# A hybrid decoder block on one core: rotary in place, another order of the second block's projections, and four smaller moves

## The chip, the cores and the metric

The kernel runs on one core of one Trainium2 chip. The metric is the device time of one execution in microseconds (us). The kernel before takes 2722.19 us, the median of three runs (2721.7 to 2723.53).

## The reference

The reference is one decoder layer for 2048 tokens of width 1024, in float32. What is touched here is the first projection and what hangs on it:

```python
h = modulate(rms_norm(x, g_pre_mix), shift_m, scale_m)
proj = h @ w_in
q_a, k_a, v_a, q_m, k_m, v_m, o_m, i_m, f_m, g_a, g_m = split(proj)
q_a, k_a = rope(q_a), rope(k_a)              # rotary on queries and keys
y_a = sliding_window_attention(q_a, k_a, v_a, sinks)   # 128-token window, softmax with a sink
qk_m = silu(causal_conv4([q_m, k_m]))
h_m = mlstm_chunkwise(q_m, k_m, v_m, i_m + b_i, f_m + b_f)
y_m = sigmoid(o_m) * head_layer_norm(h_m)
merged = sigmoid(g_a) * (y_a @ w_branch_attn) + sigmoid(g_m) * (y_m @ w_branch_mlstm)
x = x + gate_m * rms_norm(merged @ w_out)    # then the SwiGLU half, untouched here
```

`mod = c @ w_ada + b_ada` gives shifts, scales and gates. Rotary turns pairs of head columns: `[t1*cos - t2*sin, t2*cos + t1*sin]`. The mLSTM weights are `exp(d - m)` under a causal mask.

## The kernel before

The 2048 tokens are taken as two superblocks of 1024 (sb 0 and 1), each of two blocks of 512 tokens (b0 and b1; over the kernel they are blocks 0 to 3), each block of four token tiles of 128. Every float32 product is made of three fp32r matmuls: weights and activations are split into a high part (`whi`, `hl`) and a rest (`wlo`), by a copy on ScalarE (L259, L1353) and a subtraction on VectorE (L260, L1354).

A superblock's main list is written out in `superblock`: for b0 queries (C_Q, 512 columns), then keys, values and gate inputs together (264 columns), then the mLSTM values (`vm`, 512 columns); for b1 `vm` first, then queries, then keys/values. After it come the "pairs" (mLSTM q/k, output gate `om`, branch gates `ga` and `gm`), which take feature tiles of both blocks, then the outputs. `token_group` runs one such projection: four PSUM tiles `acc` (the pool has four), one per token tile, and an evacuation per tile (`evac_q` L781, `evac_kv` L805, `vm` L827: a ScalarE copy into an SBUF tile `tx`).

Beside the main list run streams: generators that were given a delay by `spawn` and are moved on by `tick` when a modelled clock has reached their time. They are the rotary tails `q_stream` and `k_stream`, the attention of a token tile (two streams, odd and even tiles), the gates' scans, the sums for the next activations, the modulation product `ada_stream`, and the mLSTM. The streams use four PSUM tiles `mix`. This fixes the order of each engine's instructions when the program is built; on the chip every engine works through its list in order and waits at semaphores.

The rotary path of a token tile: ScalarE copies the projection from `acc` to `raw` (`tx`). `rope` (L745 to L763) writes `raw*cos` to `y`, the swapped halves times sin to `z`, and adds `z` into `y`, five VectorE instructions. `q_stream` then has TensorE transpose `y` to a `mix` tile, and writes a high part (ScalarE, L771) and a rest (VectorE, L772) to `hi` and `lo`, which go to DRAM (`at_d`) by DMA; `k_stream` does the same for the keys (L796) into one tile `kk`. So a query tile takes five `tx` buffers (raw, y, z, hi, lo) and a key/value tile four. The pool has nine, given out in turn: the next tile waits for the release of the one whose buffer it gets. The attention of a token tile loads `at` from `at_d` (L908, two buffers), makes 24 score matmuls into four `mix` tiles, copies (L931), maxima, eight exponentials (L946), a reciprocal (L949), a scaling on GpSimd (L950), transposes, copies (L959), and the products with the values (PV), whose result ScalarE evacuates (L972).

In the mLSTM, `chunk_state` makes `wd` for a chunk by four VectorE instructions (add a per-row column, minimum with the mask `cneg`; L1022) and one exponential of 512 columns (L1023).

Of the kernel before, what the change touches and what calls it, by code (L numbers as in the profile page):

```python
# [71 lines left out]
def decoder_block(ctx: ExitStack, tc: tile.TileContext, a: dict, out: bass.AP, dbg=None):  # L72
# [27 lines left out]
    def mix_tile():  # L100
        return ps_mix.tile([P, 512], F32, tag="mix", name=nm("mix"))

    def tx(shape, dtype=F32):
        return tpool.tile(shape, dtype, tag="tx", name=nm("tx"), bufs=9)

    def tm(shape, dtype=F32):
        return mpool.tile(shape, dtype, tag="tm", name=nm("tm"), bufs=9)
# [202 lines left out]
    def token_group(srcs, nk, n, lhs, evac, pair_heads=False, stagger=1):  # L310

        acc = []
        srcs = list(srcs)
        held = []

        def make(si, k0, kc):
            def mms(wt):
                if not acc:
                    acc.extend(acc_tile() for _ in range(NT))
                held.append((wt, k0, kc))  # L320
                if len(srcs) - stagger <= si < len(srcs) - 1:
                    return
                for t in range(NT):
                    for w_, k0_, kc_ in held:
                        for j in range(kc_):
                            kk = k0_ + j
                            mm3(acc[t][:, :n], lhs(kk, t), (w_[0][:, j, :], w_[1][:, j, :]), kk == 0, kk == nk - 1)
                            yield
                    if si == len(srcs) - 1:
                        evac(t, acc[t])  # L330
                held.clear()
            return mms

        for si, (raw, view, k0, kc) in enumerate(srcs):
            yield piece(raw, view, [kc, n], make(si, k0, kc), pair_heads)
# [400 lines left out]
    def superblock(sb):  # L736
# [9 lines left out]
        def rope(raw, heads, b, t):  # L746
            sin, cos = tables[sb]
            t += (b % 2) * NT
            W = heads * HD
            raw = raw[:, :W]  # L750
            src = raw.rearrange("p (h u f) -> p h u f", u=2, f=32)
            cb = cos[:, t, :].unsqueeze(1).to_broadcast([P, heads * 2, 32])
            sb_ = sin[:, t, :].unsqueeze(1).to_broadcast([P, heads, 32])
            y = tx([P, W])
            z = tx([P, W])
            zz = z.rearrange("p (h u f) -> p h u f", u=2, f=32)
            yy = y.rearrange("p (h u f) -> p h u f", u=2, f=32)
            V.tensor_tensor(y.rearrange("p (h f) -> p h f", f=32), raw.rearrange("p (h f) -> p h f", f=32), cb, op=ALU.mult)
            V.tensor_tensor(zz[:, :, 0, :], src[:, :, 1, :], sb_, op=ALU.mult)
            V.tensor_tensor(zz[:, :, 1, :], src[:, :, 0, :], sb_, op=ALU.mult)  # L760
            V.tensor_tensor(yy[:, :, 0, :], yy[:, :, 0, :], zz[:, :, 0, :], op=ALU.subtract)
            V.tensor_tensor(yy[:, :, 1, :], yy[:, :, 1, :], zz[:, :, 1, :], op=ALU.add)
            return y  # L763

        def q_stream(b, t, y):
            yield L_ROPE
            pt = mix_tile()
            for j in range(GQ):
                transpose(pt[:, j * P:(j + 1) * P], y[:, j * P:(j + 1) * P])
            hi, lo = tx([P, 512], F32R), tx([P, 512], F32R)  # L770
            A.activation(hi, pt, AF.Copy, scale=HD ** -0.5)  # L771
            V.scalar_tensor_tensor(lo, pt, HD ** -0.5, hi.bitcast(F32), op0=ALU.mult, op1=ALU.subtract)  # L772
            for i, q in enumerate((hi, lo)):
                nc.sync.dma_start(at_d[b * NT + t][:, i * 512:(i + 1) * 512], q.bitcast(F32))
# [13 lines left out]
            nc.sync.dma_start(raw[:, :, 256:], w_in[:, C_IF:C_IF + 8].rearrange("(k p) c -> p k c", p=P))  # L788
            return raw

        def k_stream(n, y):
            yield L_ROPEK
            pt = mix_tile()
            transpose(pt[:, :P], y)
            kk = tx([P, 2, P], F32R)
            A.copy(kk[:, 0, :], pt[:, :P])  # L796
            V.tensor_tensor(kk[:, 1, :], pt[:, :P], kk[:, 0, :].bitcast(F32), op=ALU.subtract)
            for n_, u in ((n, 1), (n + 1, 0)):
                if n_ < S // P:
                    nc.sync.dma_start(at_d[n_][:, AT_K:AT_V].rearrange("p (i u k) -> p i u k", i=2, u=2)[:, :, u, :], kk.bitcast(F32))  # L800
# [16 lines left out]
            return evac  # L817

        def q_kv(b):
            yield from token_group(srcs_rows(w_in, KD, C_Q), KD, 512, lhs_h(b), evac_q(b), pair_heads=True)  # L820
            raw_kv = Raw(load_kv)
            yield from token_group([(raw_kv, (lambda r, j=j: r[:, j:j + 2, :]), j, 2) for j in range(0, KD, 2)], KD, 264, lhs_h(b), evac_kv(b))

        def vm(b):
            def evac(t, ps):
# [175 lines left out]
        def chunk_state(c):  # L1001
            b, t = b0 + c // NT, c % NT
            negm_d, mp, cl, ex = R["gates", b]
            cs = slice(t * P, (t + 1) * P)
            n_ = b * NT + t
            Cnew = c_tile(n_ + 1)
            km, qm = ld([MH, P]), ld([MH, P])
            nc.sync.dma_start(km, qk_d[b][:, 1, :, cs])
            nb = tm([P, MH, P])
            nc.sync.dma_start(nb, negm_d[:, cs].unsqueeze(0).to_broadcast([P, MH, P]))  # L1010
            nc.sync.dma_start(qm, qk_d[b][:, 0, :, cs])
            vc = vmt[n_ % 2]
            nc.sync.dma_start(vc[:, :, :MD], vm_d[b][:, t, :].rearrange("p (h d) -> p h d", h=MH))
            yield L_LOAD
            pk = mix_tile()
            for hh in range(MH):
                transpose(pk[:, hh * P:(hh + 1) * P], km[:, hh, :])
            kw = tm([P, MH, P])
            V.tensor_tensor(kw, pk.rearrange("p (h d) -> p h d", h=MH), ex[:, 0, t, :].unsqueeze(2).to_broadcast([P, MH, P]), op=ALU.mult)
            wd = tm([P, MH, P])  # L1020
            for hh in range(MH):
                V.scalar_tensor_tensor(wd[:, hh, :], nb[:, hh, :], cl[:, t, 0, hh:hh + 1], cneg, op0=ALU.add, op1=ALU.min)  # L1022
            A.activation(wd, wd, AF.Exp)  # L1023
            qs_ = None
            if n_ > 0:
                qs_ = tm([P, MH, P])
                G.tensor_tensor(qs_, nb, mp[:, :, t].unsqueeze(2).to_broadcast([P, MH, P]), op=ALU.add)
                A.activation(qs_, qs_, AF.Exp)
                G.tensor_tensor(qs_, qs_, qm, op=ALU.mult)
            R["w", c] = wd, qs_, km, qm, vc  # L1030
            yield L_KW
            pcn = [mix_tile() for _ in range(2)]
            for hh in range(MH):
                mm(pcn[hh // 2][:, (hh % 2) * 129:(hh % 2) * 129 + 129], kw[:, hh, :], vc[:, hh, :], True, True)
            for hh in range(MH):
                o = pcn[hh // 2][:, (hh % 2) * 129:(hh % 2) * 129 + 129]
                if n_ == 0:
                    V.tensor_copy(Cnew[:, hh, :], o)
                else:
                    V.scalar_tensor_tensor(Cnew[:, hh, :], C[n_][:, hh, :], ex[:, 2, t, hh:hh + 1], o, op0=ALU.mult, op1=ALU.add)  # L1040
# [238 lines left out]
            hps[b1] = spawn(hprep(b1), L_HP2)  # L1279

        yield start
        yield from q_kv(b0)
        yield lambda: attend(b0)
        if sb == 0:
            yield lambda: R.update(ada_m=[spawn(ada_stream([(2, "gate")], 5000.0))])
        yield from vm(b0)
        yield lambda: finish([hps[b1]])
        yield lambda: hps.update(t=spawn(hsums(("T2", "T4"))))
        yield from vm(b1)
        yield from q_kv(b1)  # L1290

        def start_f():
            finish([hps["t"]])
# [2 lines left out]
            attend(b1)  # L1296

        yield start_f
        pairs = [("qk", 0), ("om", 0), ("qk", 1), ("om", 1), ("qk", 2), ("ga", 0), ("qk", 3), ("ga", 1),
                 ("ga", 2), ("ga", 3), ("gm", 0), ("gm", 1), ("gm", 2), ("gm", 3)]  # L1300
        for i, (kind, p) in enumerate(pairs):
            parts = list(in_pair(kind, p))
            if i == 0:
                yield from parts[:3]
                yield lambda: finish([hps["t"]])
                parts = parts[3:]
            if i + 1 == len(pairs):
                yield from parts[:2]
                yield lambda: end_attention(NT)
                yield lambda: (load_y(b0, 0), load_g(b0, 0))  # L1310
                parts = parts[2:]
            yield from parts
            if (kind, p) == ("ga", 1):
                yield lambda: finish(convs + R["gs", b0] + R["gs", b1])
                yield lambda: spawn(mlstm(), L_ML)
        yield from outputs(b0)
# [550 lines left out]
```

## Time and profile before

| | before |
|---|---|
| median of three runs | 2722.19 us |
| the profiled execution | 2727.14 us |
| its span | 2725.4 us |
| TensorE (PE) busy | 2644.5 us, 97% |
| VectorE / ScalarE / GpSimd busy | 73% / 47% / 6% |
| DMA moved | 511.89 MB, mean 188 GB/s |

The profiled execution lies 4.95 us above the median of the runs, and its span 1.74 us below its own time. PE is busy for 97% of the span, so what can change the time is PE's work, its clock, and the 81 us in which it stands idle. About 33 us of these lie in the first 66 us (24.4) and the last 35 us (9.0) of the span.

### The profile page before, as it was taken

To read this page: it belongs to the slowest core of one execution; us is meant where nothing else is said; L and a number is where in the kernel's file an instruction comes from. 1 tells how busy PE (TensorE), PEld (TensorE's weight loads), DVE (VectorE), ACT (ScalarE), POOL (GpSimd) and SP (SyncE) were. 2 spreads that over 40 slices of the span, in tenths; PEclk is the share of its full clock that TensorE was granted. 3 is DMA by queue.
4 is the path that set the end of the run, shared out by engine and by line. 5 is a ranking of instruction groups with operands and counts; after the bars stand their busy time and mean duration, and the time that the engine had idled before them with its cause. 6 is when DMAs were issued, how large, how long until landed. Compare 5 with 4: busy or idle time off the path is not lost.

```text
span 2725.4 us, 35775 instructions
## 1 busy us (share of the span) xinstructions
PE 2644.5 (97%) x12310; PEld 2136.0 (78%) x12310; DVE 1999.1 (73%) x3954; ACT 1287.0 (47%) x2510; POOL 152.6 (6%) x189
## 2 busy tenths in 40 slices
PE   6999999999989899999999999999999999999998
PEld 4767778888877677888887888888877888888886
DVE  7959877866786988876587777776677676766456
ACT  5555743444755564334563443335554333333444
POOL 2010101100101010110000000000000000000000
PEclk8999999999999999999999999999999999999999
DMA  7755445697675554568765664436675332324566
GB/s 248 234 154 179 147 136 168 206 333 255 219 231 187 177 160 153 180 218 315 255 198 199 198 192 155 147 121 213 204 272 194 102 115 86 112 93 147 185 210 216
DMA packets 353639, 511.89 MB, mean 188 GB/s; under 512 B 25121, under 2 KB 213661, under 8 KB 348209
## 3 DMA queue, kind: packets, MB, share of 16 engines
q1 hardware_dynamic: 353456, 509.61, 56.6%
q8 instruction: 97, 1.59, 0.2%
q14 instruction: 86, 0.70, 0.1%
HBM read 357.12 MB, written 144.02 MB: 184 GB/s over the span
## 4 chain that ended last, share of the span: by engine, by line
PE 77%; DVE 7%; issue 4%; DMA 2%; ACT 2%; POOL 0%; SPq 0%; DVEq 0%; POOLq 0%; ACTq 0%
PE acc L204 54%; PE mix L204 22%; DVE hl L1354 1%; PE mix L209 1%; ACT hl L1353 1%; DMA at_d<-tx 1%; DMA raw<-as_d 1%; DVE tx L1132 1%; DMA raw<-in_w_ffn_down_dram 1%; DMA raw<-ws_d 0%; DVE w L1664 0%; DVE big L1354 0%; DVE big L552 0%; POOL rs L475 0%; DMA x1n<-tm 0%
## 5 line engine op out<-in xcount | busy, mean ns | idle before, releaser
L204 PE MATMUL acc<-big,hl 128*128 128x512 f32 x3936 | 947.7, 394 | 13.7 <-ACT tx L805 5.9
L204 PEld LDWEIGHTS acc<-big,hl 128*128 128x128 f32 x3936 | 732.8, 189 | 183.3 <-issue 10.2
L1353 ACT CAST hl<-raw 128x512 fp32r<-128x512 f32 x732 | 439.4, 621 | 500.5 <-PE acc L204 233.0
L1354 DVE TENSOR_TENSOR hl<-raw,hl 128x512 fp32r<-128x512 f32 x732 | 495.8, 694 | 193.6 <-ACT hl L1353 192.6
L204 PE MATMUL acc<-whi,big 128*128 128x512 f32 (+1 forms) x1280 | 380.8, 378 | 19.0 <-ACT big L518 8.4
L204 PEld LDWEIGHTS acc<-whi,big 128*128 128x128 f32 x1280 | 236.4, 192 | 65.9 <-ACT big L518 8.5
L204 PE MATMUL mix<-big,hl 128*128 128x512 f32 x1056 | 263.9, 390 | 1.6 <-ACT hl L1353 1.0
L204 PE MATMUL acc<-wlo,big 128*128 128x512 f32 (+1 forms) x640 | 241.8, 380 | 3.4 <-DVE wlo L260 3.4
L204 PE MATMUL acc<-hl,hl 128*128 128x512 f32 x1008 | 237.0, 393 | 4.7 <-DVE hl L1354 2.9
L204 PEld LDWEIGHTS mix<-big,hl 128*128 128x128 f32 x1056 | 197.7, 188 | 46.0 <-DVE hl L1354 1.8
L204 PEld LDWEIGHTS acc<-hl,hl 128*128 128x128 f32 x1008 | 187.1, 188 | 49.8 <-DVE hl L1354 8.4
L204 PE MATMUL mix<-hl,hl 128*128 128x512 f32 x792 | 183.2, 391 | 2.3 <-ACT hl L1353 1.4
L204 PEld LDWEIGHTS mix<-hl,hl 128*128 128x128 f32 x792 | 147.7, 188 | 37.0 <-DVE hl L1354 3.3
L260 DVE TENSOR_TENSOR wlo<-raw,whi 128x1024 fp32r<-128x1024 f32 (+1 forms) x96 | 108.8, 1133 | 71.8 <-ACT whi L259 65.1
L259 ACT CAST whi<-raw 128x1024 fp32r<-128x1024 f32 (+1 forms) x96 | 94.5, 985 | 128.6 <-PE acc L204 123.2
L204 PE MATMUL acc<-big,whi 128*128 128x512 f32 x512 | 154.9, 391 | 0.0
L204 PEld LDWEIGHTS acc<-wlo,big 128*128 128x128 f32 x640 | 123.1, 192 | 29.6 <-DVE wlo L260 5.1
L475 POOL TENSOR_TENSOR rs<-ms,nhalf 128x1 f32<-128x1 f32 (+1 forms) x56 | 42.7, 774 | 1642.4 <-DVE ms L473 1639.7
L204 PE MATMUL mix<-hcT4h,hl 128*128 128x512 f32 x352 | 117.6, 394 | 0.7 <-ACT hl L1353 0.7
L204 PE MATMUL acc<-hcT2h,hl 128*128 128x512 f32 x352 | 117.5, 394 | 0.0
L204 PEld LDWEIGHTS acc<-big,whi 128*128 128x128 f32 x512 | 95.7, 188 | 19.6
L204 PE MATMUL acc<-big,wlo 128*128 128x512 f32 x256 | 96.3, 392 | 0.0
(331 smaller groups left out, 3482.3 us busy)
## 6 DMA issues: line engine op xcount, KB each, us to landing
raw<-in_w_in_dram SPq DMA_DIRECT2D x48, 1024.0 KB
as_d<-w SPq DMA_DIRECT2D x154, 256.0 KB
raw<-as_d SPq DMA_DIRECT2D x70, 512.0 KB
raw<-in_w_ffn_gate_dram SPq DMA_DIRECT2D x22, 1024.0 KB
raw<-in_w_ffn_up_dram SPq DMA_DIRECT2D x22, 1024.0 KB
raw<-ws_d SPq DMA_DIRECT2D x40, 512.0 KB
tx<-in_w_ada_dram SPq DMA_DIRECT2D x64, 256.0 KB
y_d<-tm SPq DMA_DIRECT2D x64, 256.0 KB
```

Source lines behind the costliest of these rows:

```text
L204: T.matmul(o, lhsT=lhsT, rhs=rhs, start=start, stop=stop, skip_group_check=resumed)
L209: T.transpose(o, i, ident[:k, :k])
L259: A.copy(hv, src)
L260: V.tensor_tensor(lv, src, hv.bitcast(F32), op=ALU.subtract)
L475: G.tensor_tensor(r[:, :n], ms[:, :n], nhalf[:, :n], op=ALU.pow)
L1132: V.scalar_tensor_tensor(ac, u[:, j:j + TB], col("conv_w", j * 8 + f), ac, op0=ALU.mult, op1=ALU.add)
L1353: A.copy(v(hi), src)
L1354: V.tensor_tensor(v(lo), src, v(hi).bitcast(F32), op=ALU.subtract)
```

## The change

Six edits. (1) `rope` works in place: `raw` takes the place of `y`, and `z` is always a 512-column tile. `hi` and `lo` of the queries are written into `z` and `raw`, and `kk` into the unused columns of `z`. Two `tx` buffers a tile, for queries and for keys/values, but they stay taken until the DMAs to `at_d` have read them. (2) In b1 the order of the three projections is keys/values, queries, `vm`. (3) The stream of the modulation product for the mixer's gate starts at the fifth pair and not ahead of b0's `vm`, with a gap of 6000 ns on the model clock and not 5000. (4) The pairs begin with the output gate, and (5) the mLSTM is spawned behind ("qk", 3), at the same place in the list. (6) `wd` is one masked addition of 512 columns on VectorE and four exponentials of 128 columns with the column as bias.

```diff
-            y = tx([P, W])
-            z = tx([P, W])
-            zz = z.rearrange("p (h u f) -> p h u f", u=2, f=32)
-            yy = y.rearrange("p (h u f) -> p h u f", u=2, f=32)
-            V.tensor_tensor(y.rearrange("p (h f) -> p h f", f=32), raw.rearrange("p (h f) -> p h f", f=32), cb, op=ALU.mult)
+            z = tx([P, 512])
+            zz = z[:, :W].rearrange("p (h u f) -> p h u f", u=2, f=32)
+            rr = raw.rearrange("p (h f) -> p h f", f=32)
             V.tensor_tensor(zz[:, :, 0, :], src[:, :, 1, :], sb_, op=ALU.mult)
             V.tensor_tensor(zz[:, :, 1, :], src[:, :, 0, :], sb_, op=ALU.mult)
-            V.tensor_tensor(yy[:, :, 0, :], yy[:, :, 0, :], zz[:, :, 0, :], op=ALU.subtract)
-            V.tensor_tensor(yy[:, :, 1, :], yy[:, :, 1, :], zz[:, :, 1, :], op=ALU.add)
-            return y
+            V.tensor_tensor(rr, rr, cb, op=ALU.mult)
+            V.tensor_tensor(src[:, :, 0, :], src[:, :, 0, :], zz[:, :, 0, :], op=ALU.subtract)
+            V.tensor_tensor(src[:, :, 1, :], src[:, :, 1, :], zz[:, :, 1, :], op=ALU.add)
+            return raw, z
...
-            hi, lo = tx([P, 512], F32R), tx([P, 512], F32R)
+            hi, lo = z.bitcast(F32R), y.bitcast(F32R)
...
-            kk = tx([P, 2, P], F32R)
+            kk = z[:, P:3 * P].bitcast(F32R).rearrange("p (i k) -> p i k", i=2)
...
+            V.tensor_tensor(wd, nb, cneg.unsqueeze(1).to_broadcast([P, MH, P]), op=ALU.add)
             for hh in range(MH):
-                V.scalar_tensor_tensor(wd[:, hh, :], nb[:, hh, :], cl[:, t, 0, hh:hh + 1], cneg, op0=ALU.add, op1=ALU.min)
-            A.activation(wd, wd, AF.Exp)
+                A.activation(wd[:, hh, :], wd[:, hh, :], AF.Exp, bias=cl[:, t, 0, hh:hh + 1])
...
-        if sb == 0:
-            yield lambda: R.update(ada_m=[spawn(ada_stream([(2, "gate")], 5000.0))])
         yield from vm(b0)
         yield lambda: finish([hps[b1]])
         yield lambda: hps.update(t=spawn(hsums(("T2", "T4"))))
+        q1, kv1 = (list(z) for z in q_kv(b1))
+        yield from kv1
+        yield from q1
         yield from vm(b1)
-        yield from q_kv(b1)
...
-        pairs = [("qk", 0), ("om", 0), ("qk", 1), ("om", 1), ("qk", 2), ("ga", 0), ("qk", 3), ("ga", 1),
+        pairs = [("om", 0), ("qk", 0), ("om", 1), ("qk", 1), ("ga", 0), ("qk", 2), ("ga", 1), ("qk", 3),
...
+            if sb == 0 and i == 4:
+                yield lambda: R.update(ada_m=[spawn(ada_stream([(2, "gate")], 6000.0))])
...
-            if (kind, p) == ("ga", 1):
+            if (kind, p) == ("qk", 3):
```

What this makes of the engines' lists is shown at two places, both in superblock 0 while b1's projections run beside the attention of b0's tiles. First TensorE, in the kernel before, from the last score matmuls of b0's token tile 3 (`mix_1504<-at_1390`) on; `acc_1812` and `acc_1813` are b1's query projections of its token tiles 2 and 3. Twelve matmuls of `acc_1980` and `acc_1981` (keys/values) follow these rows, and then the transposes of token tile 2.

```order
L204 MATMUL mix_1503<-at_1390 128x256
L204 MATMUL mix_1504<-at_1390 128x256
L204 MATMUL acc_1812<-wlo_1875,big_691 128x512
L204 MATMUL acc_1812<-whi_1874,big_692 128x512
L204 MATMUL acc_1812<-whi_1874,big_691 128x512
L204 MATMUL acc_1812<-wlo_1875,big_691 128x512
L204 MATMUL acc_1812<-whi_1874,big_692 128x512
L204 MATMUL acc_1813<-whi_1874,big_691 128x512
```

The same place on TensorE in the changed kernel: `mix_1466` and `mix_1467` hold token tile 3's last scores, `mix_1522` and `mix_1552` tile 2's transposes, `mix_1567` its PV, `mix_1578` and `mix_1596` tile 3's transposes, `mix_1614` its PV, and `mix_1797` and `mix_1806` the transposes of b1's keys.

```order
L204 MATMUL mix_1466<-at_1359 128x256
L204 MATMUL mix_1467<-at_1359 128x256
L209 MATMUL mix_1522<-ident,tm_1368 128x128 x4
L209 MATMUL mix_1552<-ident,tm_1369 128x128 x4
L204 MATMUL mix_1567<-tm_1527,at_1328 64x512
L204 MATMUL mix_1567<-tm_1557,at_1328 64x512
L204 MATMUL mix_1567<-tm_1529,at_1328 64x512
L204 MATMUL mix_1567<-tm_1559,at_1328 64x512
L209 MATMUL mix_1578<-ident,tm_1446 128x128 x4
L209 MATMUL mix_1596<-ident,tm_1447 128x128 x4
L204 MATMUL mix_1614<-tm_1583,at_1359 64x512
L209 MATMUL mix_1797<-ident,tx_1704 128x128
```

Between tile 3's scores and tile 2's transposes no projection matmul stands any more; the next ones, `acc_1973` (`vm` of b1's token tile 1), stand behind all of tile 3's PV and three of the key transposes.

Second, ScalarE at the same place. In the changed kernel, from token tile 2's copies (`tm_1527`, `tm_1557`) on: the exponentials of token tile 3 (`tm_1446`, `tm_1447`), its copies, the high parts of b1's keys (L797) and the evacuation of b1's second query tile (`tx_1930`).

```order
L959 COPY tm_1527<-mix_1522 128x512
L959 COPY tm_1557<-mix_1552 128x512
L946 ACTIVATE tm_1446,sums_1444<-tm_1446,nmx_1443 128x128
L942 ACTIVATE es_1445<-es_1445 128x8
L946 ACTIVATE tm_1446,sums_1444<-tm_1446,nmx_1443 128x128 x3
L946 ACTIVATE tm_1447,sums_1444<-tm_1447,nmx_1443 128x128 x4
L972 CAST tm_1572<-mix_1567 128x512
L959 COPY tm_1583<-mix_1578 128x512
L959 COPY tm_1601<-mix_1596 128x512
L797 CAST tx_1706<-mix_1797 128x128
L797 CAST tx_1728<-mix_1806 128x128
L781 COPY tx_1930<-acc_1789 128x512
```

In the kernel before, ScalarE has there, from tile 2's second copy (`tm_1599`) on, the evacuations of b1's third and fourth query tiles, after tile 3's copies (`tm_1622`, `tm_1640`).

```order
L959 COPY tm_1599<-mix_1594 128x512
L972 CAST tm_1611<-mix_1606 128x512
L959 COPY tm_1622<-mix_1617 128x512
L959 COPY tm_1640<-mix_1635 128x512
L972 CAST tm_1655<-mix_1650 128x512
L781 COPY tx_1949<-acc_1812 128x512
L781 COPY tx_1967<-acc_1813 128x512
```

The evacuation of b1's second query tile has moved from ahead of the attention of tiles 2 and 3 to behind it and behind two key transposes; tile 3's exponentials have moved from ahead of tile 2's second copy to behind it. The same rows stand in superblock 1.

More of the change, by code (lines that the diff above doesn't have):

```diff
@@ L753, in rope, with q_stream @@
             sb_ = sin[:, t, :].unsqueeze(1).to_broadcast([P, heads, 32])
-            y = tx([P, W])
-            z = tx([P, W])
-            zz = z.rearrange("p (h u f) -> p h u f", u=2, f=32)
-            yy = y.rearrange("p (h u f) -> p h u f", u=2, f=32)
-            V.tensor_tensor(y.rearrange("p (h f) -> p h f", f=32), raw.rearrange("p (h f) -> p h f", f=32), cb, op=ALU.mult)
+            z = tx([P, 512])
+            zz = z[:, :W].rearrange("p (h u f) -> p h u f", u=2, f=32)
+            rr = raw.rearrange("p (h f) -> p h f", f=32)
             V.tensor_tensor(zz[:, :, 0, :], src[:, :, 1, :], sb_, op=ALU.mult)
             V.tensor_tensor(zz[:, :, 1, :], src[:, :, 0, :], sb_, op=ALU.mult)
-            V.tensor_tensor(yy[:, :, 0, :], yy[:, :, 0, :], zz[:, :, 0, :], op=ALU.subtract)
-            V.tensor_tensor(yy[:, :, 1, :], yy[:, :, 1, :], zz[:, :, 1, :], op=ALU.add)
-            return y
-        def q_stream(b, t, y):
+            V.tensor_tensor(rr, rr, cb, op=ALU.mult)
+            V.tensor_tensor(src[:, :, 0, :], src[:, :, 0, :], zz[:, :, 0, :], op=ALU.subtract)
+            V.tensor_tensor(src[:, :, 1, :], src[:, :, 1, :], zz[:, :, 1, :], op=ALU.add)
+            return raw, z
+        def q_stream(b, t, yz):
             yield L_ROPE
+            y, z = yz
             pt = mix_tile()
@@ L789, in load_kv, with k_stream @@
             return raw
-        def k_stream(n, y):
+        def k_stream(n, yz):
             yield L_ROPEK
+            y, z = yz
             pt = mix_tile()
             transpose(pt[:, :P], y)
-            kk = tx([P, 2, P], F32R)
+            kk = z[:, P:3 * P].bitcast(F32R).rearrange("p (i k) -> p i k", i=2)
             A.copy(kk[:, 0, :], pt[:, :P])
@@ L819, in q_kv @@
         def q_kv(b):
-            yield from token_group(srcs_rows(w_in, KD, C_Q), KD, 512, lhs_h(b), evac_q(b), pair_heads=True)
             raw_kv = Raw(load_kv)
-            yield from token_group([(raw_kv, (lambda r, j=j: r[:, j:j + 2, :]), j, 2) for j in range(0, KD, 2)], KD, 264, lhs_h(b), evac_kv(b))
+            return token_group(srcs_rows(w_in, KD, C_Q), KD, 512, lhs_h(b), evac_q(b), pair_heads=True), token_group([(raw_kv, (lambda r, j=j: r[:, j:j + 2, :]), j, 2) for j in range(0, KD, 2)], KD, 264, lhs_h(b), evac_kv(b))
         def vm(b):
@@ L1281, in superblock @@
         yield start
-        yield from q_kv(b0)
+        for z in q_kv(b0):
+            yield from z
         yield lambda: attend(b0)
-        if sb == 0:
-            yield lambda: R.update(ada_m=[spawn(ada_stream([(2, "gate")], 5000.0))])
         yield from vm(b0)
```

## The prediction

> **What bounds the kernel now.** I read the page first, for the engine that sets the time and for its clock; then the waits of TensorE, for who stops it; then busy time by windows, for where; and at last the timelines of those places. From the page:
>
> ```profile
> span 2725.4 us, 35775 instructions
> PE 2644.5 (97%) x12310; PEld 2136.0 (78%) x12310; DVE 1999.1 (73%) x3954; ACT 1287.0 (47%) x2510; POOL 152.6 (6%) x189
> PEclk8999999999999999999999999999999999999999
> ```
>
> TensorE (PE) is the bound nearly everywhere, at a clock that falls under nine tenths in one slice alone. The change takes no matmul away, so it can move only PE's 81 us of idle time and what PE loses at a lower clock. Who stops PE, by line:
>
> ```profile
> engine line waited for: us in total, times, longest us
> PE acc L204 <- ACT tx L805: 8.7, 5, 4.3
> ...
> PE acc L204 <- ACT tx L781: 4.0, 3, 2.2
> PE acc L204 <- ACT tx L827: 3.8, 3, 2.0
> PE acc L204 <- DVE wlo L260: 3.4, 2, 2.2
> ```
>
> The evacuations of keys/values (L805), queries (L781) and vm (L827) come late 16.5 us in all: the stages that the change reorders. By windows (busy us of each engine, PE's clock, DMA share, GB/s):
>
> ```profile
> 66.00:94.00 28.00, 24.43 (x167) 22.64 (x166) 28.00 (x60) 18.70 (x31) 0.94 (x2) 0.94 0.42 144
> 112.00:165.00 53.00, 49.41 (x225) 36.39 (x223) 33.92 (x77) 27.51 (x75) 4.16 (x4) 0.94 0.76 245
> 165.00:198.00 33.00, 29.98 (x165) 19.14 (x165) 18.74 (x48) 15.54 (x54) 4.85 (x5) 1.00 0.36 106
> 198.00:234.00 36.00, 27.46 (x135) 21.77 (x135) 31.75 (x91) 16.48 (x35) 0.00 (x0) 0.86 0.68 221
> 756.00:812.00 56.00, 49.13 (x278) 42.16 (x277) 47.79 (x123) 30.92 (x53) 0.00 (x0) 0.97 0.67 216
> 882.00:960.00 78.00, 68.09 (x343) 50.90 (x342) 74.97 (x194) 49.87 (x123) 8.34 (x7) 1.00 0.54 181
> 341.00:749.00 408.00, 408.00 (x1968) 339.27 (x1967) 303.72 (x658) 199.84 (x358) 42.81 (x42) 1.00 0.65 219
> 1088.00:1260.00 172.00, 172.00 (x906) 146.43 (x905) 134.51 (x347) 72.08 (x129) 27.02 (x22) 1.00 0.70 226
> ```
>
> A window's loss is its length less PE's busy time, plus busy time x (1 - clock). Superblock 0, b0 (66 to 94): 3.6 + 1.5 = 5.0 us. Its b1 (112 to 234): idle 3.6 + 3.0 + 8.5 = 15.1, clock 3.0 + 3.8 = 6.8, together 21.9. Superblock 1, b0 (756 to 812): 6.9 + 1.5 = 8.4. Its b1 (882 to 960): 9.9. So 45.2 us can be won here at most. The last two rows, pairs and mLSTM, have no PE idle time.
>
> **The change, part by part.** *Two buffers a tile.* The rotation keeps five VectorE instructions of the same sizes, so it costs nothing itself; what moves is when a `tx` buffer comes free. In superblock 1's b0 that is what stops PE now:
>
> ```profile
> 762.82 0.39 PE L204 MATMUL acc<-whi,big 128*128 128x264 f32 x1 [2.15 <-ACT tx L781]
> 788.19 0.50 PE L204 MATMUL acc<-whi,big 128*128 128x512 f32 x1 [1.98 <-ACT tx L805]
> 806.56 0.50 PE L204 MATMUL acc<-whi,big 128*128 128x512 f32 x1 [2.04 <-ACT tx L827]
> ```
>
> ```profile
> 787.76 0.38 ACT L805 COPY tx<-acc 128x264 f32<-128x264 f32 x1 [5.65 <-DMA at_d<-tx]
> ```
>
> ```profile
> 803.85 2.18 ACT L551 CAST big<-big 128x512 fp32r<-128x512 f32 x4 [3.47 <-DMA big<-big]
> ```
>
> ScalarE stood 5.65 us for a buffer that a DMA to `at_d` still read; eight of nine buffers now hold four whole tiles, so the first two waits should go. At 806.56 the evacuation L827 stood behind L551, which waited for a DMA; in the new list b0's four L827 stand ahead of L551. I leave 2.5 of 8.4 us: **-6** (bounds -8.4, and 0 if the buffers' DMAs remain late). In superblock 0's b0 the waits are others:
>
> ```profile
> 78.33 0.39 PE L204 MATMUL acc<-wlo,big 128*128 128x264 f32 x1 [2.23 <-DVE wlo L260]
> ```
>
> There an L260 stands behind three and a half rotations on VectorE, and behind all four in the new list, two instructions more, some 0.7 us; the later evacuations win a little: **-1** (bounds -3 to +2).
>
> *The order of b1.* Gone with it is the stretch that now ends superblock 0's b1:
>
> ```profile
> 214.16 0.80 PE L204 MATMUL acc<-big,hl 128*128 128x512 f32 x1 [4.28 <-ACT tx L805]
> ```
>
> ```profile
> 219.03 0.38 ACT L805 COPY tx<-acc 128x264 f32<-128x264 f32 x1 [4.92 <-DMA at_d<-tx]
> ```
>
> Keys/values come last in it, their evacuations wait for buffers, and the pairs behind wait for `acc`. In the new order `vm` is last, its evacuations need a buffer each and no rotation, and rotations and gates lie beside its matmuls; I leave 1.4 us. Three things take its place.
>
> First, keys/values at the head are 264-column matmuls, which use up weights about twice as fast, while the gates' scans of b0 and the splits of other activations stand ahead of the `wlo` parts on VectorE. I price that by its like at 78.33: 2.2 us, with 1.5 us of clock in superblock 0 (bounds 0 and 5).
>
> Second, and largest, the place shown in the change's section: four kv tiles take eight of nine `tx` buffers, b1's first query tile the ninth, and the second query evacuation needs one that a key transpose must free. Those transposes stand behind the attention of tiles 2 and 3 in PE's list, and `vm` behind them. So PE has nothing beside the softmax of these two tiles. What it had there before:
>
> ```profile
> 176.91 1.69 PE L204 MATMUL mix<-at 64*128 64x256 f32 x24
> ...
> 187.35 0.66 PE L209 MATMUL mix<-ident,tm 128*128 128x128 f32 x4 [1.23 <-POOL tm L950]
> 187.93 1.93 PE L204 MATMUL mix<-tm,at 128*64 128x512 f32 x6
> ...
> 194.74 1.07 PE L204 MATMUL mix<-tm,at 128*64 128x512 f32 x2
> ```
>
> ```profile
> 171.71 0.97 PE L204 MATMUL mix<-at 64*128 64x256 f32 x6
> ```
>
> ```profile
> 178.50 1.04 POOL L950 TENSOR_TENSOR tm<-tm,sums 128x512 f32<-128x512 f32 x1 [26.72 <-DVE sums L949]
> 180.09 1.21 POOL L950 TENSOR_TENSOR tm<-tm,sums 128x512 f32<-128x512 f32 x1 [0.55 <-ACT tm L931]
> ```
>
> ```profile
> 178.72 0.39 ACT L946 ACTIVATE tm<-tm,nmx 128x128 f32<-128x128 f32 x1
> ```
>
> Tile 2's scores ended at 172.7, its two scalings on GpSimd at 179.5 and 181.3: 6.9 and 8.6 us later. In the new list tile 3's eight exponentials (0.39 us each) stand behind tile 2's last copy: about 8.6 + 0.7 (transposes) + 0.6 (copy) = 9.9; plus 3.1 of exponentials and some 1.4 of reciprocal and scaling: 14.4; transposes, copy and the last PV bring `vm` to 17 us after the scores. PE's own work in that time: 1.7 of scores, 4 x 0.66 of transposes, about 2 x 2.9 of PV (1.07 and 1.93 a tile, overlapping) and half a microsecond for keys: 10.6. So at least 6.4 us of idle time. With engines that also do other work the whole took 18.9 us, from 178.6 to 195.8 in tile 3, and 1.7 of its scores ahead: 8.3 us idle. I take 9, between this and what a late `at` adds, plus 2.4 of clock, in each superblock (bounds 6.4, and 21 by rival (b)). As to the late `at`: its load now has 1.6 us of scores and six matmuls of 0.23 us on PE ahead of its use, and the nearest row, with its issue, says
>
> ```profile
> 915.44 0.97 PE L204 MATMUL mix<-at 64*128 64x256 f32 x12 [1.86 <-DMA at<-at_d]
> ```
>
> ```profile
> 910.17 0.40 SPq L908 DMA_DIRECT2D at<-at_d  x1
> ```
>
> 5.3 us from issue to use, so tile 3's scores may wait 2.3 us (5.3 less 3.0); most of this falls inside tile 2's softmax.
>
> The clock's price is from these rows, the stretch ahead and the stretch behind two waits:
>
> ```profile
> 128.00:130.00 2.00, 0.96 (x7) 1.00 1.04 376
> 130.00:136.00 6.00, 6.00 (x17) 0.52 0.58 158
> ...
> 786.00:788.00 2.00, 0.21 (x2) 1.00 0.07 24
> 788.00:792.00 4.00, 3.81 (x11) 0.63 0.27 92
> ```
>
> After about 2 us of idle time in three the clock is 0.52 over 6 us and 0.63 over 4 us: 2.9 and 1.4 us lost; I take 2.4 for a longer stall. The Trainium skill ("TensorE: Matmul & The Clock Gate", Part 1, the two states) lets the clock fall only after at least one idle window of about 3.4 us. By it a stall in pieces of 2 to 3 us would keep full clock, and the 2.4 us in each superblock would go: about 2710 and not 2715. The rows above speak against it, since the idle stretches there were shorter; half clock for about 3.4 us or a multiple agrees.
>
> Third, b1's `vm` weights load later and keys/values earlier; that moves SP's loads, but no row shows PE waiting for a weight load there, so nothing (bounds -1, +2).
>
> Superblock 0's b1 after: 3.7 + 11.4 + 1.4 = 16.5, before 21.9: **-5.5**. Superblock 1's b1: 2.2 + 11.4 + 1.4 = 15, before 9.9: **+5**.
>
> *The rest.* `wd`: in 16 chunks four VectorE instructions become one, and one exponential four.
>
> ```profile
> L1023 ACT ACTIVATE tm<-tm x16: 632/642/652, 402.3 to 1234.2; 128x512 f32<-128x512 f32 x16
> ```
>
> By the 0.39 of an exponential of 128 columns that is 4 x 0.39 - 0.64 = 0.9 us a chunk on ScalarE, 14.7 us in all, beside PE at 408.00 of 408.00 and ScalarE at 200 of 408: nothing. The gate stream leaves superblock 0's projections for the pairs, where the same rows show full cover, and the pairs' order keeps PE's matmuls; nothing (bounds -2, +4).
>
> Sum: -6 - 1 - 5.5 + 5 = -7.5 us. The profiled execution took 2727.14 us (span 2725.4 and 1.7 around it), which is 4.95 above the median; 2727.1 - 7.5 - 4.95 = 2714.7: **2715 us**. Less than 0.2% (5.4 us) can hardly be told from no change.
>
> **Rivals.** (a) *The new stall takes what the old waits give.* At 15 us a superblock, and not 11.4, the sum is -0.3: 2722. For it: the slow clock would lie over PV and transposes. Against: 15 needs the chain to last as long as before among other work. (b) *Slower: the softmax of two tiles in series, with nothing beside it.* If the whole takes 18.9 us again, a late `at` adds 2.3 in front, and PE's 10.6 us run at half clock, a superblock loses 18.9 + 2.3 - 10.6 + 10.6 = 21.2 us, 9.8 more than I count: 2 x 9.8 - 7.5 = +12.1, 2734. It decides from 17.9 us a superblock on, where the sum passes +5.4. For it: rows of PE in exactly that order; against: ScalarE and VectorE are then almost free. (c) *The stall is short.* With 6.4 us of idle time and no slow clock it is 5 less in each superblock, and with b0's waits wholly gone 3 more: 2702. For it: the sums from rows; against: they have no waits between engines in them. (d) *No slow clock behind the stall*, because it comes in pieces: 2 x 2.4 less, 2710; the rows at 130 and 788 speak against it. That the buffers do not relieve b0 lies inside (a).
>
> **Chances.** Forecast (2708 to 2720) 0.36, (a) 0.17, (b) 0.26, (c) 0.16, (d) 0.05. A quarter of the forecast's weight is within 5.4 us, as is (a). Faster by over 0.2%: 0.27 + 0.16 + 0.05 = 0.48; within 0.2%: 0.09 + 0.17 = 0.26; slower: 0.26. The range reaches from (c) with all of it gone, 2698, to (b) with half the bound of the pairs, 2736; the forecast's own is 2708 to 2720.
>
> **What would show it.** Superblock 1's b0 with no wait above 1 us for L781 and the kv evacuation; PE busy after 198 to 234 without the 4.28; between the scores of tile 3 and b1's second `vm` tile a row of waits for POOL L950 and L959 that sums to about 9 us, in both superblocks, and clock 0.5 behind it. I am wrong if those waits sum to under 5 or over 13, if keys/values at the head of b1 wait for `wlo` by more than 5 us, or if the pairs show idle time.

## The result and the profile after

The changed kernel takes 2711.34 us, the median of six runs (2709.75 to 2716.59); the kernel before takes 2722.48 us in six runs, the three above among them. The ratio is 0.996 with a 95% interval of 0.9948 to 0.9971: faster by 11 us. The profiled execution has a span of 2714.9 us, 10.5 less than before; like that of before it lies about 5 us above its median, so the two traces can be set side by side. From the page of the changed kernel, the span and TensorE's line:

```profile
span 2714.9 us, 35793 instructions
PE 2639.2 (97%) x12310; PEld 2138.9 (79%) x12310; DVE 1986.2 (73%) x3906; ACT 1299.8 (48%) x2558; POOL 148.2 (5%) x189
```

Idle time has fallen from 81 to 76 us, and busy time by 5 us with the same 12310 matmuls. Who stops TensorE in the changed kernel (us in total, times, longest):

```profile
PE acc L204 <- DVE wlo L260: 6.4, 8, 2.1
PE mix L209 <- DVE tm L933: 5.9, 2, 4.1
PE mix L209 <- POOL tm L950: 5.4, 6, 1.4
PE mix L204 <- DMA at<-at_d: 5.2, 2, 2.7
...
PE acc L204 <- ACT tx L827: 3.2, 2, 1.8
```

The evacuations of queries and of keys/values, 12.7 us before, no longer stand there. In their place are parts of the attention: its load `at`, its masked scores (L933), its scaling (L950). By windows, at the places of the changed kernel:

```profile
66.00:94.00 28.00, 25.46 (x179) 23.14 (x178) 27.79 (x64) 20.28 (x34) 1.17 (x2) 1.00 0.44 142
...
158.00:192.00 34.00, 27.14 (x134) 15.91 (x133) 20.91 (x58) 17.41 (x59) 4.68 (x5) 0.90 0.49 152
192.00:234.00 42.00, 41.97 (x221) 33.92 (x220) 36.32 (x79) 25.98 (x55) 0.00 (x0) 1.00 0.64 227
741.00:784.00 43.00, 40.13 (x244) 35.05 (x243) 37.13 (x104) 21.95 (x37) 0.00 (x0) 1.00 0.62 189
784.00:820.00 36.00, 33.40 (x212) 29.40 (x210) 33.83 (x106) 22.06 (x61) 1.91 (x2) 0.95 0.72 258
820.00:870.00 50.00, 40.58 (x186) 24.65 (x184) 26.73 (x70) 25.47 (x79) 7.29 (x8) 0.83 0.43 134
```

The end of superblock 0's b1 (192 to 234) is full now, where before PE stood 8.5 us. Two holes are new: 6.9 us in 158 to 192 and 9.4 us in 820 to 870, at clocks of 0.90 and 0.83.

Windows compare badly where work moves between stages. So for all runs I took TensorE's matmuls one by one: the time from one's start to the next one's start, less the median of that time for its shape in the kernel before, summed over stages that are cut at equal amounts of matmul work. This is the loss, idle time and slow clock together. In us, from one profiled execution each (one execution lies up to 5 us off its kernel's median, and that shows here too: e8's edits lie behind b1 of superblock 0, and it loses 19.0 there where the trace of before has 24.7; and a wait that lies on a cut falls to one stage or the other):

| kernel | sb 0, b0 | sb 0, b1 | sb 0, rest | sb 1, b0 | sb 1, b1 | its first pairs | median, us |
|---|---|---|---|---|---|---|---|
| before | 6.2 | 24.7 | 1.3 | 9.8 | 5.9 | 3.4 | 2722.5 |
| changed | 3.7 | 10.8 | 0.7 | 4.7 | 18.8 | 3.2 | 2711.3 |
| e1: rotary | 5.0 | 19.3 | 3.2 | 3.4 | 5.5 | 9.3 | 2728.5 |
| e5: gate stream | 6.2 | 4.4 | 3.6 | 9.1 | 4.5 | 8.2 | 2715.1 |
| e6: rotary, gate stream | 3.8 | 6.6 | 1.6 | 3.3 | 6.3 | 5.1 | 2706.0 |
| e2: all but the order | 3.8 | 6.6 | 2.9 | 6.2 | 9.5 | -1.7 | 2702.3 |
| e7: all but the gate stream | 4.6 | 20.9 | 0.0 | 5.4 | 15.4 | 0.5 | 2720.5 |
| e4: all but the rotary | 6.3 | 15.9 | 0.5 | 9.7 | 13.5 | -1.2 | 2720.2 |
| e8: gate first, mask | 6.3 | 19.0 | 2.4 | 8.7 | 5.8 | 1.3 | 2721.1 |
| e3: keys/values, values, queries | 3.8 | 4.7 | -0.4 | 5.7 | 8.1 | 0.3 | 2700.1 |

So, by these two traces, the changed kernel wins 13.9 us in superblock 0's b1 (8.2 against e8's trace), 5.1 in superblock 1's b0 and 2.5 in superblock 0's b0, and gives 12.7 back in superblock 1's b1 and behind it. Which edit wins and which gives back, the traces of the two kernels alone do not say; the experiments do.

### The profile page after: what moved, and what is told of

It is laid out like the page before. It is cut to its first block, busy times and chain, and to the rows that moved or that the text cites. A ratio compares the mean times of both kernels' runs of the same rounds, so it can differ in the third digit from the quotient of the medians.

```text
span 2714.9 us, 35793 instructions
## 1 busy us (share of the span) xinstructions
PE 2639.2 (97%) x12310; PEld 2138.9 (79%) x12310; DVE 1986.2 (73%) x3906; ACT 1299.8 (48%) x2558; POOL 148.2 (5%) x189
## 4 chain that ended last, share of the span: by engine, by line
PE 85%; DVE 7%; DMA 4%; ACT 2%; issue 1%; POOL 0%; SPq 0%; DVEq 0%; ACTq 0%; POOLq 0%
PE acc L204 61%; PE mix L204 22%; PE mix L209 2%; DVE hl L1357 1%; DVE tm L428 1%; DMA raw<-as_d 1%; ACT tm L946 1%; ACT hl L1356 1%; DMA raw<-in_w_in_dram 1%; DMA at_d<-tx 0%; DMA big<-in_x_dram 0%; DVE wlo L260 0%; DMA tx<-in_w_ada_dram 0%; DVE w L1667 0%; DMA at<-at_d 0%
## 5 line engine op out<-in xcount | busy, mean ns | idle before, releaser
L204 PE MATMUL acc<-whi,big 128*128 128x512 f32 (+1 forms) x1280 | 379.3, 377 | 10.8 <-ACT big L518 8.4
L260 DVE TENSOR_TENSOR wlo<-raw,whi 128x1024 fp32r<-128x1024 f32 (+1 forms) x96 | 109.0, 1137 | 65.5 <-ACT whi L259 59.8
```

What stands on the lines that cost most here:

```text
L204: T.matmul(o, lhsT=lhsT, rhs=rhs, start=start, stop=stop, skip_group_check=resumed)
L260: V.tensor_tensor(lv, src, hv.bitcast(F32), op=ALU.subtract)
```

## The experiments

The theory at the start (A): the buffers pay by themselves, and the order pays in superblock 0 and costs in superblock 1. The rival (B): the order pays, and the buffers only make it possible.

**e1, the in-place rotary alone**, with the old order: the diff's lines in `rope`, `q_stream` and `k_stream`, nothing else.

> The kernel before with the in-place rotary alone (two temporaries a tile), old order of b1, nothing else. Theory A, the buffers pay by themselves: the two b0 stages lose 2.6 and 5.8 us less, as in the changed kernel, and b1's key/value evacuations at the end of the old order no longer wait for buffers, some 5 us more in each superblock; about 2706 to 2714 us. Rival B, the order of b1 pays and the buffers only make it possible: 2718 to 2722, as before within noise, with the 4 us wait for the key/value evacuation still there at the end of superblock 0's b1.

2728.45 us, ratio to the kernel before 1.0022 (95% interval 1.0013 to 1.003; so for each run below): slower, which neither had. Both b0 stages lose less (5.0 and 3.4), so the buffers do what they should there. b1 of superblock 0 still loses 19.3 us, as in e8 (19.0). TensorE and, below, ScalarE in it:

```profile
116.91 0.50 PE L204 MATMUL acc<-whi,big 128*128 128x512 f32 x1 [3.66 <-ACT tx L828]
```

```profile
111.73 2.18 ACT L551 CAST big<-big 128x512 fp32r<-128x512 f32 x4 [1.58 <-DMA big<-big]
114.20 2.18 ACT L551 CAST big<-big 128x512 fp32r<-128x512 f32 x4 [0.29 <-DMA big<-big]
116.28 1.06 ACT L828 COPY tx<-acc 128x512 f32<-128x512 f32 x2
```

The values' evacuation stands behind eight casts of the next activations (L551), which wait for their load. In the list of before three of the four evacuations stood ahead of them, here one, and PE waits 3.7 us. More is lost later, 9.3 us in superblock 1's first pairs; what starts that was not followed.

**e2, the changed kernel with the old order of b1.**

```diff
-        yield from kv1
-        yield from q1
         yield from vm(b1)
+        yield from q1
+        yield from kv1
```

> The changed kernel with only the order of b1's projections put back (values, queries, keys/values). Theory A: the stall beside the softmax of token tiles 2 and 3 (6.8 us in superblock 0, 10.4 in superblock 1) goes, and what the order won at the end of b1 comes back in part; within 4 us of e1, 2704 to 2714. Rival B: the old losses of b1 come back whole (25 and 10 us against 11 and 22 now): 2713 or more.

2702.3 us, ratio 0.9922 (0.9908 to 0.9935): 9 us faster than the changed kernel, below what A gave. In the changed kernel the new order costs, and B is gone for it. But e2 stands 26 us below e1, and the two differ only in the gate stream, the pairs' order and the mask, the three edits priced at nothing.

**e3, the changed kernel with keys/values, mLSTM values, queries in b1.**

```diff
         yield from kv1
-        yield from q1
         yield from vm(b1)
+        yield from q1
```

> The changed kernel with b1's order keys/values, mLSTM values, queries. The values' evacuation needs one buffer that a DMA frees at once, so projection matmuls stand again between the scores of tile 3 and the transposes of tile 2. If the stall is made by queries waiting for buffers that key transposes must free: the stall goes, and the kernel takes 2694 to 2704, unless the queries at the end of b1 wait in their turn (then 2706 to 2712). Rival C, the stall is the load of the attention tile and the softmax itself, whatever stands beside: 2709 to 2713, with waits for the load, the scaling and the copies of 7 to 10 us in each superblock as in the changed kernel.

2700.08 us, ratio 0.9918 (0.9904 to 0.9932), the fastest of all, level with e2. The same places in e3, by windows:

```profile
158.00:200.00 42.00, 39.76 (x191) 26.31 (x189) 27.51 (x59) 25.96 (x76) 5.15 (x5) 1.00 0.52 173
820.00:880.00 60.00, 57.52 (x260) 36.95 (x260) 35.52 (x83) 31.77 (x85) 4.69 (x5) 1.00 0.59 181
```

2.2 and 2.5 us idle where the changed kernel has 6.9 and 9.4, and full clock. The attention is the same, its load too; so C is out. With projection matmuls beside it the softmax of two tiles costs nearly nothing.

**e4, the changed kernel with the old rotary**: `rope`, `q_stream` and `k_stream` of the kernel before.

> The changed kernel with the old rotary (five and four temporaries), the new order and everything else kept. Theory A: the b0 stages get their losses back (2.6 + 5.8), and b1, where four key/value tiles now need sixteen buffers, stalls at least as long: 2718 to 2730. Rival B, the order pays: 2711 to 2716.

2720.19 us, ratio 0.9989 (0.998 to 0.9998): the in-place rotary is worth 8.9 us here, where alone it cost 6. The b0 stages have their old losses back (6.3 and 9.7).

The next four look for the 26 us. Theory G: the gate's modulation stream, which ran beside b1 of superblock 0, is what b1 suffered from. Its rival H: only stream and rotary together count.

**e5, the gate stream's move alone.**

```diff
-        if sb == 0:
-            yield lambda: R.update(ada_m=[spawn(ada_stream([(2, "gate")], 5000.0))])
         yield from vm(b0)
...
             parts = list(in_pair(kind, p))
+            if sb == 0 and i == 4:
+                yield lambda: R.update(ada_m=[spawn(ada_stream([(2, "gate")], 6000.0))])
```

> The kernel before with only the gate's modulation stream moved to the fifth pair. Theory G, that stream is what b1's projections of superblock 0 suffer from (each of its 18 loads takes a buffer of the ring and some of the DMA's time, beside evacuations that need buffers): the 26.7 us that superblock 0's b1 loses fall by some 10 us even with the old rotary; 2708 to 2716. Rival H, it needs both, since with four and five buffers a tile the ring is short with or without the stream: 2719 to 2724.

2715.14 us, ratio 0.9974 (0.9964 to 0.9985): 7.6 us faster by two moved lines. b1 of superblock 0 loses 4.4 us; a part of the gain is lost again in superblock 1's first pairs (8.2).

**e6, the rotary and the gate stream**, and nothing else (e1's and e5's diffs).

> The kernel before with the in-place rotary and the gate's stream moved; old order of b1, old order of the pairs, old masked exponential. If these two edits carry the whole gain of e2 (2702.3): 2700 to 2705. If the output gate first or the single masked addition has a share: 2707 or more.

2706.04 us, ratio 0.9941 (0.9929 to 0.9954): 16.7 us, more than the sum of the two alone (+5.5 and -7.6). The rotary is worth 9 us once the stream is away. e6 is 3.7 us above e2, with intervals that overlap.

**e7, the changed kernel with the gate stream put back** (e5's diff reversed).

> The changed kernel with only the gate's stream put back ahead of b0's mLSTM values. Theory G: superblock 0's b1 loses its gain, 10 to 16 us; 2721 to 2728. Rival: keys/values first frees b1 from that stream, and the time stays at 2709 to 2714.

2720.5 us, ratio 0.9991 (0.9982 to 1.0): nearly the whole gain of the change is gone with this one edit, 9.2 us, a little less than G had. b1 of superblock 0 loses 20.9 us, and its longest wait, TensorE's row here, is e1's again:

```profile
116.01 0.59 PE L204 MATMUL acc<-whi,big 128*128 128x264 f32 x1 [3.80 <-ACT tx L827]
```

Beside e1 (2728.45 us) e7 shows a second thing. Both have the new rotary and the stream in its old place, and they differ in the order of b1, the pairs' order and the mask; e7 is 8.0 us faster, and e8, next, puts the last two at nothing. So with the stream in place the new order wins about what it costs with the stream away. The traces do not show where: b1 of superblock 0 loses 20.9 us in e7 and 19.3 in e1, and the profiled execution of e7 lies 5 us above its median.

**e8, the output gate first and the masked addition**, on the kernel before.

> The kernel before with only the pairs' order (output gate first, the mLSTM's start moved by name) and the single masked addition with four exponentials. The prediction's terms for both were nothing: 2719 to 2725, TensorE without idle time in the pairs and the mLSTM. Were they to matter, 5 us or more either way.

2721.09 us, ratio 0.9994 (0.9986 to 1.0003): no change that can be told, as predicted.

The last four ask what of the stream costs, and what makes the stall.

**e9, the gate stream in other buffers**, on the kernel before.

```diff
-                    raw = tx([P, 1, 512])
+                    raw = ld([1, 512]) if parts[0][0] == 2 else tx([P, 1, 512])
```

> The kernel before, with the gate's stream where it was, but its loads into the mLSTM's four load buffers (idle in this stage) and not into the ring of nine. If the ring is what the stream costs: b1 of superblock 0 gains what e5 gained (26.7 to about 16 us of loss), 2711 to 2717. If it is the DMA's time or VectorE's terms: 2719 to 2724.

2721.68 us, ratio 0.9996 (0.9987 to 1.0005): no gain. The ring of nine buffers by itself is not what the stream costs.

**e10, a narrow gate stream**, on the kernel before.

```diff
+                w = 64 if part == 2 else 512
+                if part == 2:
+                    V.memset(acc, 0.0)
...
-                    nc.sync.dma_start(raw, w_ada[:, c0:c0 + 512].rearrange("(p k) c -> p k c", k=KD)[:, k:k + 1, :])
+                    nc.sync.dma_start(raw[:, :, :w], w_ada[:, c0:c0 + w].rearrange("(p k) c -> p k c", k=KD)[:, k:k + 1, :])
                     yield gap
-                    ada_terms(acc, raw, k, 1)
+                    ada_terms(acc[:, :w], raw[:, :, :w], k, 1)
```

> The kernel before, with the gate's stream where it was and in the ring's buffers, but loading and multiplying only 64 of each 512 columns (the rest of the gate is left zero, so this part of the computation is missing): the buffers are taken as before, an eighth of the DMA's bytes and a part of VectorE's time. If the ring alone counts: 2719 to 2724. If DMA and VectorE count: 2711 to 2717, and ScalarE's 4 us wait for the other activations' load at 126 us is gone.

2724.11 us, ratio 1.0006 (0.9998 to 1.0015): no gain either. In its trace b1 of superblock 0 loses 11.8 us, less than before, but b0 ahead of it 8.8 and superblock 1's first pairs 6.5. So neither buffers alone nor bytes and VectorE's time alone account for the stream. Left are both together, the accumulator `tm` that the stream holds through eight loads out of the nine that the attention uses, and where its instructions push others in the lists; none of these was tried alone, and the cause inside the stream stays open.

**e11, the changed kernel with key/value temporaries in the mLSTM's load buffers**, so that the ring has five buffers left for queries and values and not one.

```diff
-            z = tx([P, 512])
+            z = tx([P, 512]) if heads == HQ else ld([1, 512])[:, 0, :]
```

> The changed kernel with the second temporary of the key/value tiles taken from the mLSTM's load buffers, so that four key/value tiles hold four of the ring's nine buffers and not eight. If b1's stall is the second query evacuation waiting for a buffer that a key transpose must free: query and value matmuls stand beside the softmax of tiles 2 and 3, the losses of 6.8 and 12.8 us there fall under 4 each, and the time is 2698 to 2704. If the stall is the attention's own (its load, its softmax): 2709 to 2713.

2724.22 us, ratio 1.0008 (0.9999 to 1.0017): 13 us slower than the changed kernel, which neither side had. The stall in superblock 0 is gone, 0.24 and 0.36 us of waits between 150 and 185 are all; so there it was the ring. In superblock 1 it stays (TensorE's row):

```profile
865.22 1.12 PE L209 MATMUL mix<-ident,tm 128*128 128x128 f32 x4 [4.88 <-POOL tm L950]
```

Elsewhere it loses: superblock 0's b0 9.3 us against 3.7, and from 120 to 160 TensorE is as busy as in the changed kernel (39.98 and 40.00 us), but at a clock of 0.83 and not 0.99. The two profiled executions are only 5.3 us apart (2721.86 and 2716.59), so the traces hold less than half of the 13 us.

**e12, e3 with the same buffers** (e3's and e11's diffs).

> e3's order (keys/values, mLSTM values, queries) with the same own buffers. If buffers still cost anything in e3 (queries' evacuations at the end of b1, 2 us, and the first stage): 2694 to 2699. If e3 has no loss left that buffers make: 2698 to 2702, as e3.

2710.57 us, ratio 0.9961 (0.9949 to 0.9974): 10.5 us slower than e3, by more buffers. From the pages of e3 and, below, of e12:

```profile
span 2697.3 us, 35742 instructions
PE 2630.7 (98%) x12310; PEld 2129.7 (79%) x12310; DVE 1988.4 (74%) x3906; ACT 1301.2 (48%) x2558; POOL 152.7 (6%) x189
```

```profile
span 2708.9 us, 35728 instructions
PE 2642.4 (98%) x12310; PEld 2140.9 (79%) x12310; DVE 1986.4 (73%) x3906; ACT 1300.9 (48%) x2558; POOL 150.8 (6%) x189
```

TensorE is idle for 66.6 us in e3 and for 66.5 in e12. With the same 12310 matmuls it is busy 11.7 us longer, and so the loss is its clock: the mean granted clock is 0.990 to 0.992 in the five executions of e12, and 0.995 or 0.996 in the four of e3. What starts a first slow stretch stands in b0, on VectorE. The split of the values' second weights in e3, and below in e12, with TensorE's waits there:

```profile
90.83 1.21 DVE L260 TENSOR_TENSOR wlo<-raw,whi 128x1024 fp32r<-128x1024 f32 x1
```

```profile
94.98 1.23 DVE L260 TENSOR_TENSOR wlo<-raw,whi 128x1024 fp32r<-128x1024 f32 x1
```

```profile
94.42 0.30 PE L209 MATMUL mix<-ident,tx 128*128 128x128 f32 x1 [1.79 <-DVE tx L761]
96.27 0.50 PE L204 MATMUL acc<-wlo,big 128*128 128x512 f32 x1 [1.55 <-DVE wlo L260]
```

VectorE is busy throughout 66 to 94 in both. With a buffer at hand for each tile, the key rotations and the activations' sums take VectorE's time ahead of the split, and PE waits for a rotation and then for weights; from 94 to 110 its clock is 0.89, in e3 1.00. In e3's list the rotations stand further behind; that the short ring put them there is argued, not shown. A longer slow stretch follows: from 120 to 160 the clock is 0.83 (e3: 1.00), behind a wait of 2.22 us for the gates' scans (L863) at 120.09. e3 has a wait of 2.05 us at 117.48 and keeps full clock behind it; why, no run shows.

## Why the prediction was right, and where it was not

2715 us was forecast and 2711.3 came, inside the forecast's own range. None of the signs of being wrong came either: the stall's waits sum to 6.75 and 9.4 us, the longest wait for `wlo` at the head of b1 is 2.05 us, and where the pairs had no idle time they still have none (400.00 of 400.00 us busy from 341 to 741). But the total is right in part by luck, as the steps show:

*Two buffers a tile, -7.* Right in the stages it named: superblock 1's b0 fell from 9.8 to 4.7 us (forecast -6), superblock 0's from 6.2 to 3.7 (forecast -1). As an edit it is worth 9 us (e5 to e6, e4 to the changed kernel), but only with the gate stream away; with the stream in place it cost 5.5 us (e1), and that was not foreseen.

*The order of b1: -5.5 in superblock 0 and +5 in superblock 1.* The step fails as put. In the changed kernel the order costs 9.0 us (e2 to the changed kernel), with the old rotary some 5 (e5 to e4); only with the gate stream in its old place does it win, 8.0 (e1 to e7). Superblock 0's b1 did gain, and more than forecast (13.9, or 8.2 against e8's trace), but the gain is the gate stream's: with the old order it is larger (6.6 us lost in e2 and e6, 10.8 in the changed kernel). The stretch at the end of b1, which I credited to the order, shrinks without it, too.

*The new stall, 9 us idle and 2.4 of clock in each superblock.* The mechanism is right, as e3 shows, and in superblock 0 the size nearly. TensorE in the changed kernel, from the last scores of token tile 2 on, superblock 0:

```profile
163.51 0.97 PE L204 MATMUL mix<-at 64*128 64x256 f32 x6
167.22 1.70 PE L204 MATMUL mix<-at 64*128 64x256 f32 x24 [2.75 <-DMA at<-at_d]
170.71 1.39 PE L209 MATMUL mix<-ident,tm 128*128 128x128 f32 x8 [1.79 <-DVE tm L933]
172.07 4.09 PE L204 MATMUL mix<-tm,at 128*64 128x512 f32 x8
177.59 0.65 PE L209 MATMUL mix<-ident,tm 128*128 128x128 f32 x4 [1.42 <-POOL tm L950]
179.03 1.04 PE L209 MATMUL mix<-ident,tm 128*128 128x128 f32 x4 [0.79 <-POOL tm L950]
...
184.47 0.48 PE L204 MATMUL acc<-whi,big 128*128 128x512 f32 x1
```

20.0 us from the end of the scores (164.5) to the next projection matmul, where I had 17. The waits sum to 6.75 us; the other 13.2 are PE's own work, which I had at 10.6, so I put 2.6 down to the clock. Idle and clock make 9.4, against 11.4. The load of `at` was late by 2.75 us (2.3 in the text); it set the start of tile 3's chain, while tile 2's went faster than before. Superblock 1:

```profile
841.08 2.74 PE L204 MATMUL mix<-at 64*128 64x256 f32 x24 [2.43 <-DMA at<-at_d]
845.10 2.93 PE L204 MATMUL mix<-at 64*128 64x256 f32 x24 [1.28 <-DVE tm L933]
852.09 2.24 PE L209 MATMUL mix<-ident,tm 128*128 128x128 f32 x8 [4.06 <-DVE tm L933]
854.26 4.37 PE L204 MATMUL mix<-tm,at 128*64 128x512 f32 x8
859.32 0.65 PE L209 MATMUL mix<-ident,tm 128*128 128x128 f32 x4 [0.68 <-POOL tm L950]
860.90 0.66 PE L209 MATMUL mix<-ident,tm 128*128 128x128 f32 x4 [0.93 <-POOL tm L950]
```

9.4 us of waits, about the 9 that I took, and here scores, transposes and PV all run slowly: 24 scores take 2.74 us and not 1.69. The window's clock is 0.83, which over 40.58 busy us makes 6.9 us where I had 2.4: that term was mis-sized. It is the half-clock part of rival (b), in one superblock of two. Why superblock 1 stalls longer, and goes on stalling with the buffers of e11, is not shown.

*Keys/values at the head, 2.2 us, with 1.5 of clock in superblock 0.* In superblock 0 it came as put: PE waits 2.05 us for `wlo` (L260) at 117.70, and the clock is 0.88 from 110 to 124. In superblock 1 the size is right (784 to 820 has 2.6 us idle and 1.7 at a lower clock), but the mechanism is another: the waits for `wlo` there are 0.17 and 0.18 us, and the longest is for an evacuation of the values ahead of them:

```profile
790.68 0.39 PE L204 MATMUL acc<-whi,big 128*128 128x264 f32 x1 [1.42 <-ACT tx L827]
```

*The gate stream: nothing, bounds -2 to +4.* This is the step that failed most. I looked at where the stream goes (the pairs, full cover) and not at what it leaves. Taken away from b1 it is worth 7.6 us alone (e5), 9.2 in the changed kernel (e7), and 22 beside the rotary (e1 to e6). It stood in the trace of before: the stream's first load is issued at 109.3 us and its first term stands on VectorE at 114.2, at the head of the window with the largest loss. I put this window's loss to the order instead. So the order stood at -0.5 us in all and cost 9.0, and the stream stood at nothing and won 9.2: two errors of about 9 us that cancel, which is luck.

*Gate first, masked addition: nothing.* Right (e8).

## What to carry to other kernels

When a change moves a side stream, price the place that it leaves as carefully as the place that it goes to: here it was as large as any term. Where a scheduler writes the lists, edits do not add: with the stream in place the rotary cost 6 us and the order won 8, with it away the rotary won 9 and the order cost 9. More buffers are not safe either: four more made two kernels 10 to 13 us slower, one of them without any more idle time on TensorE, by a lower clock alone. And before an order is judged, look at what TensorE has beside each softmax: moving one projection (e3) brought another 11 us on top of the change.

## What the runs showed of the hardware

TensorE's clock, in the changed kernel, the stretches around the stalls (length, PE busy, clock, DMA share):

```profile
168.00:171.00 3.00, 1.21 (x19) 1.00 0.01 2
171.00:176.00 5.00, 4.89 (x16) 0.66 0.00 2
...
842.00:846.00 4.00, 2.72 (x26) 0.50 0.81 262
846.00:852.00 6.00, 2.03 (x20) 0.78 0.01 1
852.00:857.00 5.00, 4.87 (x15) 0.50 0.01 3
```

At this place no single wait in superblock 0 is longer than 2.75 us, and still the clock falls to 0.66 behind them; in superblock 1 it is at 0.50 after a wait of 2.43, and again after the one of 4.06. So rival (d), by which a stall in pieces keeps full clock, is out. In e3, with waits of at most 1.22 us at that place, it stays at 1.00. By these rows waits of 2 to 3 us are enough to halve the clock. Their length alone does not decide it: the wait for `wlo` in superblock 0's b0 is 2.23 us in the kernel before (at 78.33) and 2.24 us in e5 (at 78.23), and from 79 to 83 the clock is 0.57 in the first and 1.00 in the second. Nor does work bring it back at once: in e12 TensorE is busy for 15.91 of the 16 us from 120 to 136, at a clock of 0.57. What decides between these cases, no run here shows.
